# A decoder layer on one core: a simulated timeline for the scheduler's plan, a diagonal in a staging ring, shifted tiles, and a norm issued later

## The chip, the core and the metric

The kernel runs on one core of a Trainium2 chip. The metric is the device time of one execution in microseconds, as the median of repeated runs. A core has five engines that take their instructions in order: TensorE (PE, matmuls; PEld is its weight load), VectorE (DVE), ScalarE (ACT), GpSimd (POOL) and SyncE (SP, which here only issues DMAs). ACT and POOL issue DMAs too. Engines wait for each other through semaphores.

## The reference

One layer of a hybrid decoder in float32, on 1024 tokens of width 1024: a SwiGLU half, a mixer of stick-breaking attention beside a Mamba-2 state-space part (SSD), cross attention on 256 memory tokens, and a second SwiGLU half, each inside a pair of RMS norms.

```python
f = swiglu(rmsnorm(h, ffn1_pre_g), ffn1_w_gu, ffn1_w_down)
h = h + 0.5 * rmsnorm(f, ffn1_post_g)
m = hybrid_mixer(rmsnorm(h, mix_pre_g), w_in, ...)   # attention | SSD, each with a norm, then w_out
h = h + rmsnorm(m, mix_post_g)
c = memory_cross_attention(rmsnorm(h, xa_pre_g), rmsnorm(mem, mem_g), xa_wq, xa_wkv, xa_wo)
h = h + rmsnorm(c, xa_post_g)
f = swiglu(rmsnorm(h, ffn2_pre_g), ffn2_w_gu, ffn2_w_down)
h = h + 0.5 * rmsnorm(f, ffn2_post_g)
```

## The kernel before

Activations lie with features on the 128 partitions and tokens along the free axis, in two halves of 512 tokens (hh = 0, 1) and eight tiles of 128 features (d = 0 to 7). Every float32 product is made of three matmuls of a shorter type: an operand x is split into a high part (a cast, on ACT: L263 in `split`, L270 with a gain in `scaled_split`) and a low part (the rest, on DVE: L265 or L272). So "xh" and "xl" are the two parts of an activation, "whi" and "wlo" those of a weight, "hl", "dx", "ol", "atl" and the like other low or split parts. L138 is every matmul, L141 every transpose on TensorE.

The stages follow each other: the up phase of ffn1, its down product (`down_first`), the SSD with the in-projection, attention, the mixer's out-projection, cross attention (`xattn`), the up phase of ffn2 and its down product. In both up phases the larger part of the tiles is made with a scheme of seven block products (`seven`) instead of eight. It needs sums and differences of blocks: of weights on POOL (L737, into tiles "wc", then split by L263 and L265 into "whi", "wlo" or "blk") and of activations on ACT and DVE (`scale` L666, `combine` L676 and L679, into "bh" and "bl" in ffn1 and "wc" in ffn2, then split into "S", "xh", "xl"). L789 to L818, L649, L650 and L841 take products out of their banks and form the gate "ft"; L646 stores it.

**Order.** TensorE's order is written out by hand: `_pe` (L100) chains each matmul to the one before, keeps a clock of its own (`self.clock`, in ns, some 216 for a matmul of 512 columns), and runs whatever stands in `self.later` when that clock passes its time. The order on ACT, DVE, POOL and SP is chosen by the scheduler of the tile framework from its plan of the program, except that what is issued out of `self.later` keeps its place relative to its like (`kp`, L117). A tile is taken from a pool by a tag with `bufs` slots; which slot a tile gets, and so whose last reader it waits for, is part of that plan too.

**Norms.** A norm has three steps: sums of squares on ACT and DVE (`sumsq`: L378 and L381, then L382, and L384 that adds the two halves), `rms_cols`, eight small matmuls with a square root and reciprocal (L332 to L339), and `rms_rows`, which brings the factors to the partitions' layout: DVE splits them (L347, L348), writes two diagonals (L358; the first in "dg", the second in "low"), two matmuls with a matrix of ones sum them up, and ACT copies the result (L369, "rpre" or "rpost"). `post(0)` in `down_first` (L1114) does so for the first half of the tokens, by times given after the point where it is called: the columns at 12,000 ns, the rows at 15,500, and then a step every 4,700 from 17,500.

**The mixer row.** In attention's last pair of heads (p = 7), `inproj` has a ring "ev" of two slots in the pool sp. It holds keys taken out of a bank (L1719), differences of values that TensorE then transposes (L1726, the v tile), and eight raw tiles of the SSD's result that SP loads (L1790, from mix8 to mix15) and L270 and L272 split for the out-projection. `before(6)` makes the diagonals of the first mixer row (`mix_row(0)`, L1800), `before(8)` issues its product; a second row follows. Their second diagonal lies in the tile rpre0 or rpre1, which later takes the row itself.

Of the kernel before, what the change touches and what calls it, by code (L numbers as in the profile page):

```python
# [11 lines left out]
F32R = mybir.dt.float32r  # L12
# [6 lines left out]
P = 128  # L19
# [27 lines left out]
class Kern:  # L47
# [290 lines left out]
        if r2 is not None:  # L338
            self.kp(nc.vector.tensor_tensor(out=c, in0=c, in1=r2, op=ALU.mult))  # L339

    def rms_rows(self, c, home, behind=False):

        nc = self.nc
        nb = c.shape[1]
        cs = self.t(self.tp, [P, 16], F32R, "cs", bufs=1)
        ch, cl = cs[:, 0:nb], cs[:, 4 : 4 + nb]
        self.kp(nc.vector.tensor_copy(ch, c))  # L347
        self.kp(nc.vector.tensor_tensor(out=cl, in0=c, in1=ch.bitcast(F32), op=ALU.subtract))  # L348
        dg = self.t(self.tp, [P, 4, P], F32R, "dg", bufs=1)
        if isinstance(home, tuple):  # L350
            pool, tag = home
            low = self.t(pool, [P, 4, P], F32R, tag, bufs=1)[:, 0:nb, :]
        else:
            low = dg[:, nb : 2 * nb, :]
        parts = dg[:, 0:nb, :], low
        for o, x in zip(parts, (ch, cl)):
            self.kp(
                nc.vector.tensor_tensor(  # L358
                    out=o, in0=self.ident[:, :].unsqueeze(1).to_broadcast([P, nb, P]),
                    in1=x.bitcast(F32).unsqueeze(2).to_broadcast([P, nb, P]), op=ALU.mult,  # L360
                )
            )

        def product():
            ps = self.norm_bank()
            for i, x in enumerate(parts):
                self.mm(ps[:, 0 : nb * P], self.onesr, x.rearrange("p a b -> p (a b)"), i == 0, i == 1)
            r = self.t(pool, [P, H], F32, tag, bufs=1) if isinstance(home, tuple) else home
            self.kp(nc.scalar.copy(r, ps[:, 0 : nb * P]))  # L369
            return r  # L370

        return product if behind else product()
# [634 lines left out]
    def down_first(self, sp, rw, wdn, act_d, gpost, gnext):  # L1007


        nc = self.nc  # L1010
# [71 lines left out]
        accs = [self.new_accs(), None]  # L1082
# [28 lines left out]
        squares(0, 1, 4)  # L1111
        self.norm_pool = self.dnp, 4
        self.XH = [[self.t(self.xp, [P, H], F32R, f"xh{hh}{d}") for d in range(KT)] for hh in range(2)]
        self.post(0, gpost, self.C[0], gnext, step=4700, accs=accs[0], times=(12000, 15500, 17500), tail=(5500, 9000))  # L1114
        ps = banks(0)
        product(ps)
        self.norm_pool = self.msp, 1
# [534 lines left out]
    def attention(self):  # L1652
        nc, ap = self.nc, self.ap
        with self.pools("at", ["o", "a"], []) as (op, sp, pp):
# [130 lines left out]
            def before(n):  # L1785

                if n < 8:
                    k = n
                    raw = self.t(sp, [P, H], F32, "ev", bufs=2)
                    nc.sync.dma_start(out=raw, in_=self.mix_d[8 + k][:, 0:H])  # L1790
                    self.scaled_split(self.XH[0][k], self.XL[0][k], raw, self.par("ssd_norm_g", k))
                if n == 2:
                    ready.append(next(self.Wo))
                if n == 6:
                    late.append(mix_row(0))
                if n == 8:
                    late.pop()()

            def mix_row(i):
                product = self.rms_rows(self.norm_c[i][:, 0:4], (self.rp, f"rpre{i}"), True)  # L1800
                return lambda: self.mix_r.append(product())

            def scores(p, a, c):
# [138 lines left out]
            def beside():  # L1942
                late.append(mix_row(1))
                self.first = self.mix_first(ready.pop())
                for n in range(4 * MIXED):
                    if n == 2:
                        late.pop()()
                    if n == 4 * MIXED - 4:
                        ready.append(next(Wm))
                    next(self.first)  # L1950
                    yield
                yield from memory_values(*mem_prep())
# [128 lines left out]
    def xattn(self):  # L2081


        nc = self.nc
        with self.pools("xf", ["a", "b"], []) as (sp, sp2, pp):
# [23 lines left out]
            def scores(s):  # L2109

                KH, KL = K[s]
                p[s] = []
                if s % 4 == 0:
                    sc = self.t(self.rp, [P, 2, 4], F32, "sc")
                    scale[:] = sc[:, 0, :], sc[:, 1, :]
                    for x, f in zip(scale, (0.0625, -0.0625)):
                        nc.vector.tensor_scalar(out=x, in0=self.C[s // 4], scalar1=f, scalar2=None, op0=ALU.mult)
                for tb in range(4):
                    ts_ = slice(tb * P, (tb + 1) * P)
                    ps = self.t(pp, [P, 512], F32, "dn", bufs=3)[:, 0:MEM]  # L2120
                    self.mm3(ps, [(q[s][i][0][:, ts_], q[s][i][1][:, ts_], KH[:, i, :], KL[:, i, :]) for i in range(2)])
                    st = self.t(sp, [P, 2], F32, "st", bufs=4)
                    mx, sm = st[:, 0:1], st[:, 1:2]
                    e = self.t(sp, [P, MEM], F32, "p", bufs=4)
                    with self.urgent():
                        nc.vector.reduce_max(out=mx, in_=ps, axis=AX.X)
                        nc.vector.tensor_tensor(out=mx, in0=mx, in1=scale[1][:, tb : tb + 1], op=ALU.mult)
                        nc.scalar.activation(e, ps, AF.Exp, bias=mx, scale=scale[0][:, tb : tb + 1], accum_out=sm)
                        nc.vector.reciprocal(sm, sm)
                        nc.vector.tensor_scalar(out=e, in0=e, scalar1=sm, scalar2=None, op0=ALU.mult)  # L2130
                    p[s].append(e)
                    yield

            def values(s):
                VH, VL = V[s]
                if s == 0:
                    self.place(sp, 128)
                pT = [[self.t(sp, [P, H], F32R, f"pt{n}{m}", bufs=1) for m in range(2)] for n in range(2)]
                for tp in range(2):
                    tr = self.t(pp, [P, 2, 256], F32, "tr", bufs=1) if tp == 1 else self.t(self.msp, [P, 2, 256], F32, "ms", bufs=1)  # L2140
                    for m in range(2):
                        for tt in range(2):
                            self.tr(tr[:, m, tt * P : (tt + 1) * P], p[s][2 * tp + tt][:, m * P : (m + 1) * P])
                    c = slice(tp * 256, tp * 256 + 256)
                    with self.urgent():
                        for m in range(2):
                            self.split(pT[0][m][:, c], pT[1][m][:, c], tr[:, m, :])
                    yield
                for i in range(2):
                    ps = self.t(pp, [P, H], F32, "dn", bufs=3)  # L2150
                    c = slice(i * P, (i + 1) * P)
                    self.mm3(ps, [(VH[:, m, c], VL[:, m, c], pT[0][m], pT[1][m]) for m in range(2)])
                    hi = self.t(sp if s % 4 < 2 else sp2, [P, H], F32R, "oh", bufs=4)
                    lo = self.t(sp if s % 4 < 2 else sp2, [P, H], F32R, "ol", bufs=4)
                    with self.urgent():
                        self.split(hi, lo, ps)
                    o[s // 4].append((hi, lo))
                    yield

            def zip_(*gens):  # L2160
                gens = list(gens)
                while gens:
                    for x in list(gens):
                        try:
                            next(x)
                            yield
                        except StopIteration:
                            gens.remove(x)
# [24 lines left out]
            for s in range(8):  # L2193
# [19 lines left out]
                if s < 7:  # L2213
                    step = zip_(values(s), scores(s + 1))
# [5 lines left out]
                    else:  # L2220
# [3 lines left out]
                        self.merge(step, 6100, out_parts(0, 4), 5200)  # L2224
                    load(V, s + 1, "v", 1, 1)
            v = values(7)
            self.run_all(out_part(ps[0], ws[0], 1, 4, 6))
            next(v)
# [174 lines left out]
def build(arrays):  # L2403
    nc = bacc.Bacc("TRN2", target_bir_lowering=False, num_devices=1)
    ap = {
        n: nc.dram_tensor(f"in_{n}", v.shape, mybir.dt.from_np(v.dtype), kind="ExternalInput").ap()
        for n, v in arrays.items()
    }
    ap["out"] = [
        nc.dram_tensor(n, v, F32, kind="ExternalOutput").ap() for n, v in (("out_a", (H, D_MODEL)), ("out_b", (H, D_MODEL)))  # L2410
    ]
    with tile.TileContext(nc) as tc:
        Kern(nc, tc, ap).run()
    return nc

# [7 lines left out]
```

## Time and profile before

| | us |
|---|---|
| runs | 2644.43, 2643.67, 2641.38 (median 2643.67) |
| the profiled execution | 2645.18 |
| its span | 2643.4 |
| TensorE busy / idle in the span | 2576.9 / 66.5 |
| mean granted TensorE clock | 0.992 |
| POOL busy | 530.8 |

The span is what the trace covers; 1.8 us of the profiled execution lie around it. A row of the timeline gives start, duration, engine, line, operation, output and inputs, and in brackets the idle time of the engine before it with what ended it. Where matmuls overlap in the pipeline, the start to start distance counts (0.227 us for 128x512 at full clock), not the duration.

### The profile page before, as it was taken

To read this page: it belongs to the slowest core of one execution; us is meant where nothing else is said; L and a number is where in the kernel's file an instruction comes from. 1 tells how busy PE (TensorE), PEld (TensorE's weight loads), DVE (VectorE), ACT (ScalarE), POOL (GpSimd) and SP (SyncE) were. 2 spreads that over 40 slices of the span, in tenths; PEclk is the share of its full clock that TensorE was granted. 3 is DMA by queue.
4 is the path that set the end of the run, shared out by engine and by line. 5 is a ranking of instruction groups with operands and counts; after the bars stand their busy time and mean duration, and the time that the engine had idled before them with its cause. 6 is when DMAs were issued, how large, how long until landed. Compare 5 with 4: busy or idle time off the path is not lost.

```text
span 2643.4 us, 36454 instructions
## 1 busy us (share of the span) xinstructions
PE 2576.9 (97%) x12598; PEld 2135.0 (81%) x12598; DVE 1983.2 (75%) x3085; ACT 1262.9 (48%) x2276; POOL 530.8 (20%) x660
## 2 busy tenths in 40 slices
PE   8999999999999999999999998999999999999998
PEld 6788888887777778888888787887878788888887
DVE  7888787888678774777777777775448989895675
ACT  7544443545367783445554445254445433333432
POOL 1555552001100000000000001122012555542000
PEclk9999999999999999999999999999999999999999
DMA  5688887754721226433434458777667455555976
GB/s 209 238 308 302 304 282 252 255 193 158 259 79 45 71 70 196 115 99 108 109 108 115 146 178 323 252 274 252 218 230 272 167 187 203 195 180 210 347 276 218
DMA packets 225241, 528.87 MB, mean 200 GB/s; under 512 B 28064, under 2 KB 35104, under 8 KB 225056
## 3 DMA queue, kind: packets, MB, share of 16 engines
q1 hardware_dynamic: 190432, 419.56, 48.2%
q0 software_dynamic: 27424, 93.87, 9.8%
q10 hardware_dynamic: 7200, 13.11, 1.3%
q8 instruction: 99, 1.62, 0.3%
q14 instruction: 86, 0.70, 0.1%
HBM read 353.41 MB, written 152.04 MB: 191 GB/s over the span
## 4 chain that ended last, share of the span: by engine, by line
PE 79%; DVE 9%; DMA 6%; ACT 3%; issue 2%; POOL 1%; SPq 0%; DVEq 0%; ACTq 0%; POOLq 0%
PE mm L138 45%; PE dn L138 24%; PE z L138 2%; PE ms L138 2%; PE tr L141 2%; PE y L138 1%; PE ms L141 1%; DMA wraw<-act 1%; DMA raw<-act 1%; DVE hl L265 1%; DVE wlo L265 1%; PE seg L138 1%; DMA blk<-h 1%; DVE whi L265 0%; DMA oraw<-mix 0%
## 5 line engine op out<-in xcount | busy, mean ns | idle before, releaser
L138 PE MATMUL mm<-xh,whi 128*128 128x512 f32 x1288 | 511.5, 406 | 11.1 <-ACT xh L270 7.0
L138 PE MATMUL mm<-xh,wlo 128*128 128x512 f32 x1240 | 478.5, 393 | 3.2 <-DVE wlo L265 2.9
L138 PE MATMUL mm<-xl,whi 128*128 128x512 f32 x1188 | 467.8, 394 | 1.0 <-DVE xl L265 0.7
L138 PEld LDWEIGHTS mm<-xh,whi 128*128 128x128 f32 x1288 | 244.1, 189 | 53.6 <-ACT xh L270 6.9
L138 PEld LDWEIGHTS mm<-xh,wlo 128*128 128x128 f32 x1240 | 234.3, 189 | 55.3 <-DVE wlo L265 3.4
L138 PEld LDWEIGHTS mm<-xl,whi 128*128 128x128 f32 x1188 | 225.6, 190 | 34.1 <-DVE xl L265 1.8
L1823 DVE TENSOR_TENSOR_SCAN nb<-nb,begin 128x128 f32<-128x128 f32 (+7 forms) x128 | 171.7, 1352 | 55.0 <-ACT nb L1819 54.4
L1819 ACT ACTIVATE nb<-z,scale 128x128 f32<-128x128 f32 (+2 forms) x192 | 107.8, 580 | 88.8 <-PE z L138 87.7
L263 ACT CAST whi<-wraw 128x1024 fp32r<-128x1024 f32 (+1 forms) x89 | 81.2, 914 | 69.1 <-PE mm L138 39.1
L1856 POOL MEMSET ath<- 128x128 f32 x64 | 13.1, 205 | 499.0 <-PE mm L138 499.0
L265 DVE TENSOR_TENSOR wlo<-wraw,whi 128x1024 fp32r<-128x1024 f32 x61 | 74.4, 1220 | 38.3 <-ACT whi L263 38.0
L138 PE MATMUL dn<-xh,wlo 128*128 128x512 f32 x296 | 101.0, 389 | 0.0
L737 POOL TENSOR_TENSOR wc<-wraw,raw 128x512 f32<-128x512 f32 x57 | 87.5, 1535 | 66.6 <-DVE whi L265 30.7
L737 POOL TENSOR_TENSOR wc<-raw,wraw 128x512 f32<-128x512 f32 x55 | 85.5, 1555 | 66.5 <-DVE wlo L265 31.4
L819 POOL TENSOR_TENSOR ft<-ft,e 128x512 f32<-128x512 f32 x38 | 62.4, 1642 | 144.2 <-DVE e L818 85.7
L650 ACT ACTIVATE ft<-ft 128x512 f32<-128x512 f32 x88 | 55.4, 631 | 75.0 <-DVE ft L649 70.3
L263 ACT CAST ath<-tr 128x512 fp32r<-128x512 f32 (+1 forms) x107 | 58.2, 545 | 67.5 <-PE tr L141 66.1
L138 PE MATMUL dn<-xh,blk 128*128 128x512 f32 x280 | 90.2, 389 | 0.0
L265 DVE TENSOR_TENSOR atl<-tr,ath 128x512 fp32r<-128x512 f32 (+1 forms) x107 | 67.0, 629 | 29.2 <-ACT ath L263 28.9
L138 PE MATMUL dn<-xh,whi 128*128 128x512 f32 x256 | 88.0, 389 | 0.0
L138 PE MATMUL mm<-ath,v 128*128 128x256 f32 x320 | 86.2, 291 | 0.6 <-DVE sq L1838 0.6
L382 DVE TENSOR_TENSOR acc<-acc,sq 128x512 f32<-128x512 f32 x78 | 52.3, 684 | 42.5 <-ACT sq L381 42.2
(586 smaller groups left out, 6667.9 us busy)
## 6 DMA issues: line engine op xcount, KB each, us to landing
whi<-dwhi SPq DMA_DIRECT2D x57, 512.0 KB, 3.4
wlo<-dwlo SPq DMA_DIRECT2D x57, 512.0 KB, 4.2
wraw<-act SPq DMA_DIRECT2D x102, 256.0 KB, 4.4
raw<-act SPq DMA_DIRECT2D x96, 256.0 KB, 4.3
wraw<-in_w_gu SPq DMA_DIRECT2D x44, 512.0 KB, 4.4
raw<-in_w_gu SPq DMA_DIRECT2D x38, 512.0 KB, 4.8
khi<-whi POOLq DMA_DIRECT2D x30, 512.0 KB, 4.6
klo<-wlo POOLq DMA_DIRECT2D x30, 512.0 KB, 6.7
```

Source lines behind the costliest of these rows:

```text
L138: self._pe(self.nc.tensor.matmul(out, lhsT, rhs, start=start, stop=stop, skip_group_check=self.more), cost)
L141: self._pe(self.nc.tensor.transpose(out, src, self.ident if ident is None else ident), 109.0)
L263: self.kp(self.nc.scalar.copy(hi, src))
L265: (eng or self.nc.vector).tensor_tensor(out=lo, in0=src, in1=hi.bitcast(F32), op=ALU.subtract)
L382: self.kp(nc.vector.tensor_tensor(out=accs[i % 2], in0=accs[i % 2], in1=sq, op=ALU.add))
L650: nc.scalar.activation(t, t, AF.Silu)
L737: nc.gpsimd.tensor_tensor(out=t, in0=a, in1=b, op=op)
L819: nc.gpsimd.tensor_tensor(out=t1, in0=t1, in1=e, op=ALU.mult)
L1819: nc.scalar.activation(nb[:, s0:s1], z[:, 0:n], AF.Sigmoid, scale=sc[:, i : i + 1])
L1823: nc.vector.tensor_tensor_scan(out=nb[:, 0:Wd][:, ::-1], data0=nb[:, 0:Wd][:, ::-1], data1=begin[:, S - Wd : S][:, ::-1], initial=0.0, op0 ...
L1856: nc.gpsimd.memset(x[:, 0, :].bitcast(F32), 0.0)
```

## The change

Four things are changed. The tile framework's context is opened with a flag by which its scheduler makes its plan with a simulated timeline. `rms_rows` can take its second diagonal from a given pool's "ev" ring of two slots, and `mix_row` asks for that with attention's pool. `post(0)` in `down_first` issues its columns 4,500 ns later, its rows 3,000 later, starts its steps 3,000 later and makes them 400 shorter. `values` in cross attention sets aside 384 bytes a partition instead of 128, which moves the tiles allocated behind.

```diff
-    def rms_rows(self, c, home, behind=False):
+    def rms_rows(self, c, home, behind=False, at=None):
...
-            low = self.t(pool, [P, 4, P], F32R, tag, bufs=1)[:, 0:nb, :]
+            low = self.t(at or pool, [P, 4, P], F32R, "ev" if at else tag, bufs=2 if at else 1)[:, 0:nb, :]
...
-        self.post(0, gpost, self.C[0], gnext, step=4700, accs=accs[0], times=(12000, 15500, 17500), tail=(5500, 9000))
+        self.post(0, gpost, self.C[0], gnext, step=4300, accs=accs[0], times=(16500, 18500, 20500), tail=(5500, 9000))
...
-                product = self.rms_rows(self.norm_c[i][:, 0:4], (self.rp, f"rpre{i}"), True)
+                product = self.rms_rows(self.norm_c[i][:, 0:4], (self.rp, f"rpre{i}"), True, sp)
...
                 if s == 0:
-                    self.place(sp, 128)
+                    self.place(sp, 384)
...
-    with tile.TileContext(nc) as tc:
+    with tile.TileContext(nc, schedule_with_timeline_sim=True) as tc:
```

The flag changes the order on all engines but TensorE nearly everywhere: of some 3,060 rows on DVE 2,467 lines differ, on ACT 1,384 of some 2,180, on SP 978 of some 1,420, on POOL 231 of 649. TensorE keeps its sequence but for the norm that is issued later. Three places follow.

First, the mixer row (about 1470 us in the profile). The loads on SP of the raw tiles mix11 to mix14, with the semaphores that each waits for, before; "DVE" is the last reader of a slot by L272, "PE" TensorE's transposes of the v tile:

```order
L1790 DMA ev_3051_14472<-mix11_141 128x512 [waits DMAHW7_49,DMAHW1_49,DVE_49]
L1790 DMA ev_3055_14492<-mix12_142 128x512 [waits DMASW1_49,DMAHW4_49,DVE_49,PE_49]
L1790 DMA ev_3059_14509<-mix13_143 128x512 [waits DMAHW1_49,DVE_49]
L1790 DMA ev_3063_14538<-mix14_144 128x512 [waits DMAHW4_49,DVE_49,Activation_49]
L1790 DMA ev_3068_14557<-mix15_145 128x512 [waits DMAHW5_49,DMAHW3_49,DVE_49]
```

And with the change:

```order
L1790 DMA ev_3051_14472<-mix11_141 128x512 [waits DMAHW1_49,DMASW1_49,PE_49]
L1790 DMA ev_3055_14492<-mix12_142 128x512 [waits DMAHW1_49,DVE_49]
L1790 DMA ev_3059_14509<-mix13_143 128x512 [waits DMAHW4_49,DMAHW3_49,DVE_49]
L1790 DMA ev_3063_14538<-mix14_144 128x512 [waits DMAHW4_49,DVE_49]
L1790 DMA ev_3068_14557<-mix15_145 128x512 [waits DMAHW5_49,DMAHW6_49,PE_49,Activation_49]
```

The tile numbers are the same in both. Before, mix12's load waits for TensorE's transposes of the v tile, in the other slot than mix11; now it waits for DVE's read of mix11, in the same slot, and so on to mix14. On DVE, in the change, the rows from the scan (L1823) to the second split after the diagonals:

```order
L1823 SCALAR_TENSOR_TENSOR nb_3061_14530<-nb_3061_14530,begin_2088_9767 128x896
L272 SCALAR_TENSOR_TENSOR xl0_1335_6161<-ev_3051_14472,params_3_78,xh03_1248_5794 128x512
L272 SCALAR_TENSOR_TENSOR xl0_1343_6206<-ev_3055_14492,params_3_78,xh04_1249_5795 128x512
L272 SCALAR_TENSOR_TENSOR xl0_1353_6255<-ev_3059_14509,params_3_78,xh05_1250_5796 128x512
L272 SCALAR_TENSOR_TENSOR xl0_1356_6286<-ev_3063_14538,params_3_78,xh06_1251_5797 128x512
L358 TENSOR_TENSOR ev_3066_14546<-ident_36_112,cs_3064_14542 128x512
L347 CAST cs_3089_14658<-cy1_2082_9742 128x4
L348 TENSOR_TENSOR cs_3089_14658<-cy1_2082_9742,cs_3089_14658 128x4
L358 TENSOR_TENSOR dg_3090_14661<-ident_36_112,cs_3089_14658 128x512
L1823 SCALAR_TENSOR_TENSOR nb_3069_14561<-nb_3069_14561,begin_2088_9767 128x1024
L265 TENSOR_TENSOR atl_3076_14581<-tr_3074_14579,ath_3075_14580 128x512
```

The second diagonal of the first row (ev_3066) follows the L272 of mix14 (ev_3063), into the slot which that frees; before, it lay in rpre0, and none of these four L272 stood between the scan and the diagonal of the second row (dg_3090).

Second, ffn1's up phase (about 92 to 104 us). ACT's rows before; bh_295 is the last sum of activations for the product that runs, wc_309 to wc_320 are sums of weights from POOL for the next ones:

```order
L666 ACTIVATE blk_289_945<-blk_289_945,params_3_78 128x512
L263 CAST blk_301_1010<-wc_300_1008 128x512
L263 CAST xh12_14_90<-bl_290_952 128x512
L263 CAST blk_304_1029<-wc_303_1027 128x512
L263 CAST xh13_15_91<-bh_295_982 128x512
L263 CAST blk_307_1049<-wraw_278_875 128x512
L263 CAST whi_310_1070<-wc_309_1068 128x512
L263 CAST whi_317_1113<-raw2_277_873 128x512
L263 CAST wlo_313_1091<-wc_312_1089 128x512
L263 CAST wlo_321_1134<-wc_320_1132 128x512
```

And with the change:

```order
L263 CAST blk_301_1010<-wc_300_1008 128x512
L263 CAST xh12_14_90<-bl_290_952 128x512
L263 CAST blk_304_1029<-wc_303_1027 128x512
L263 CAST whi_310_1070<-wc_309_1068 128x512
L263 CAST whi_317_1113<-raw2_277_873 128x512
L263 CAST wlo_313_1091<-wc_312_1089 128x512
L666 ACTIVATE blk_289_945<-blk_289_945,params_3_78 128x512
L263 CAST wlo_321_1134<-wc_320_1132 128x512
L263 CAST xh13_15_91<-bh_295_982 128x512
L263 CAST blk_307_1049<-wraw_278_875 128x512
```

The scaling for the last sum (L666) went behind three weight casts, and its cast (xh13) behind four; on DVE its sum (L679 bh_295) stands behind the same three and its low part (xl1_31) behind the fourth.

Third, ffn2's up phase (about 2041 to 2053 us), DVE's rows with the change; ft_4351 is a gate whose second factor comes from bank mm_4361, wc_4346 and wc_4356 are sums of activations of which the next matmuls need xl0_4069 and xl0_4083:

```order
L841 TENSOR_TENSOR ft_4351_19897<-ft_4351_19897,mm_4361_19951 128x512
L265 TENSOR_TENSOR whi_4374_20026<-wraw_4332_19794,whi_4374_20026 128x512
L265 TENSOR_TENSOR S12_4276_19469<-wc_4340_19828,S12_4276_19469 128x512
L679 SCALAR_TENSOR_TENSOR wc_4341_19840<-blk_4324_19747,params_3_78,blk_4323_19744 128x512
L679 SCALAR_TENSOR_TENSOR wc_4345_19858<-blk_4324_19747,params_3_78,blk_4323_19744 128x512
L265 TENSOR_TENSOR S42_4280_19473<-wc_4341_19840,S42_4280_19473 128x512
L265 TENSOR_TENSOR S52_4284_19477<-wc_4345_19858,S52_4284_19477 128x512
L679 SCALAR_TENSOR_TENSOR wc_4346_19869<-blk_4324_19747,params_3_78,blk_4323_19744 128x512
L265 TENSOR_TENSOR xl0_4069_18937<-wc_4346_19869,xh06_1251_5797 128x512
```

Before, L841 of ft_4351 stood ten rows behind xl0_4069, between S53 (the sum after) and wc_4356; it is now ahead of S12.

## The prediction

> **What bounds it now.** I read the page first: who is busy, and of whom the chain that ended last is made.
>
> ```profile
> PE 2576.9 (97%) x12598; PEld 2135.0 (81%) x12598; DVE 1983.2 (75%) x3085; ACT 1262.9 (48%) x2276; POOL 530.8 (20%) x660
> PE 79%; DVE 9%; DMA 6%; ACT 3%; issue 2%; POOL 1%; SPq 0%; DVEq 0%; ACTq 0%; POOLq 0%
> ```
>
> TensorE is idle for 2643.4 − 2576.9 = 66.5 us, and its matmuls are not touched by the change. So the change is worth the waits that it takes from TensorE or adds to it, and what each does to the clock. The table of stretches shows the clock.
>
> ```profile
> core 0: us, PE busy (x) PEld busy (x) DVE busy (x) ACT busy (x) POOL busy (x), PEclk, DMA share, GB/s
> 84.00:97.00 13.00, 11.47 (x48) 8.10 (x46) 12.73 (x18) 7.94 (x14) 6.27 (x7) 1.00 0.78 271
> 612.00:624.00 12.00, 8.92 (x28) 6.94 (x29) 11.50 (x25) 7.83 (x15) 0.00 (x0) 0.72 0.36 111
> 1484.00:1490.00 6.00, 2.19 (x5) 1.39 (x6) 4.64 (x8) 2.65 (x4) 0.00 (x0) 0.50 0.35 97
> 1490.00:1500.00 10.00, 10.00 (x49) 8.59 (x48) 4.47 (x8) 3.62 (x8) 0.67 (x4) 0.80 0.59 190
> 1788.00:1800.00 12.00, 9.36 (x37) 7.68 (x38) 5.71 (x14) 2.49 (x6) 1.07 (x2) 0.86 0.61 208
> ```
>
> PEclk below 1 is time at half speed: a stretch of 12 us at 0.72 lost 12 × 0.28 = 3.4 us, 12 us at 0.86 lost 1.7, and after 1484 some 10 us ran at half (6 × 0.50 + 10 × 0.20 = 5.0 lost). These are the places of longer waits. In 84 to 97, DVE is busy 12.73 of 13 us: there VectorE, and not TensorE, sets the pace. ACT and DVE take their rows in order, so a row that is moved ahead and must wait holds up all rows behind it; the order of the two programs shows where that happens.
>
> **The mixer row's second diagonal (about 1470 to 1490).** Rows of the timeline and of the load's line:
>
> ```profile
> 1471.80 2.00 DVE L1823 TENSOR_TENSOR_SCAN nb<-nb,begin 128x896 f32<-128x896 f32 x1
> 1472.10 0.39 PE L138 MATMUL ms<-rpre,onesr 128*128 128x512 f32 x1
> 1473.16 0.42 PEld L141 LDWEIGHTS ms<-ident,ev 128*128 128x128 f32 x4
> 1473.74 0.65 DVE L358 TENSOR_TENSOR dg<-ident,cs 128x512 fp32r<-128x512 f32 x1
> 1483.84 0.80 PE L138 MATMUL ms<-dg,onesr 128*128 128x512 f32 x1 [1.90 <-DVE atl L265]
> 1488.45 0.79 PE L138 MATMUL ms<-rpre,onesr 128*128 128x512 f32 x1 [3.81 <-DVE rpre L358]
> 1489.04 0.63 PE L138 MATMUL mm<-xh,whi 128*128 128x512 f32 x1
> DMA to landing us min/median/max: 2.6/3.0/4.3
> L270 ACT ACTIVATE xh<-ev,params x8: 712/722/727, 1458.0 to 1486.3; 128x512 fp32r<-128x512 f32 x8
> L272 DVE SCALAR_TENSOR_TENSOR xl<-ev,params,xh x8: 724/750/752, 1459.0 to 1487.0; 128x512 fp32r<-128x512 f32 x8
> ```
>
> Before, the first row's second matmul (1472.10) waits for nothing. After, its operand is a tile of the "ev" ring, and the ring has two slots. One is held by the v tile that TensorE transposes at 1473.16, behind this matmul in its order. So the raw tiles of mix11 to mix14 and then the diagonal go through the other slot one by one: each load waits until L272 has read the tile before. The first L272 can start when the scan ends (1471.80 + 2.00) and ends at 1474.55. Then three times a landing of 3.0 us, L270's 0.72 and L272's 0.75: 3 × 4.47 = 13.4, to 1487.95; the diagonal (L358, 0.65) makes it 1488.6. TensorE is ready at 1472.10: **a wait of 16.5 us** (15.3 with landings of 2.6, 20.4 with 4.3).
>
> From 1472.10 TensorE then has 9.84 us of work up to the second row's first matmul (1483.84 less its wait of 1.90), 0.46 for that row, and about 4.5 us are lost at half clock (5.0 were lost behind the 1484 wait, which was shorter): 1488.6 + 14.8 = 1503.4 for what stood at 1489.04, +14.4. The old waits of 1.90 and 3.81 are in that difference. What half clock cost behind 1489.04 before (0.5 + 2.0) does not come again. **+12**, bounds +9.5 and +16.
>
> The Trainium skill's page "DMA: Bandwidth & Descriptors", section "Anatomy of one DMA — SWDGE (gpsimd) path", gives a fixed 2.0 us plus bytes over 436 GB/s, which for these 256 KB is an estimate of 2.6 us. The trace agrees for the quickest landing only; by the page this part would be 1.2 us cheaper, by the median row it is as above, and the row decides.
>
> **ffn1's operand sums (92 to 104).**
>
> ```profile
> 92.65 0.72 ACT L666 ACTIVATE blk<-blk,params 128x512 f32<-128x512 f32 x1 [1.99 <-DMA blk<-in_xT]
> 93.41 0.75 DVE L679 SCALAR_TENSOR_TENSOR bh<-blk,params 128x512 f32<-128x512 f32 x1
> 95.64 0.68 DVE L265 TENSOR_TENSOR xl<-bh,xh 128x512 fp32r<-128x512 f32 x1
> 96.38 0.51 PE L138 MATMUL mm<-xl,whi 128*128 128x512 f32 x1 [0.24 <-DVE xl L265]
> 98.16 1.61 POOL L737 TENSOR_TENSOR wc<-wraw,raw 128x512 f32<-128x512 f32 x1 [0.70 <-ACT whi L263]
> 98.54 1.77 DVE L265 TENSOR_TENSOR whi<-wc,whi 128x512 fp32r<-128x512 f32 x1
> 100.40 1.29 POOL L737 TENSOR_TENSOR wc<-raw,wraw 128x512 f32<-128x512 f32 x1 [0.63 <-DVE whi L265]
> 101.72 0.62 ACT L263 CAST wlo<-wc 128x512 fp32r<-128x512 f32 x1 [1.30 <-POOL wc L737]
> ```
>
> Before, the last operand sum of the product (92.65, 93.41) goes ahead of four weight casts; after, it stands behind them on both engines. The last cast needs POOL's third sum (100.40 to 101.69). It can be earlier by the two DVE rows taken out ahead of it (0.75 + 0.68 = 1.4): it ends at 100.3, the cast at 100.9, then xh (0.62) and xl behind a wlo row (0.68 to 1.77, then 0.68) end at 102.3 to 103.4. TensorE took it at 96.38: **+6.4** at a start near 102.8 (bounds +5 and +8.5, the latter with no earlier POOL). Half clock behind such a wait costs at least 1.7, as at 1788: together **+8**, bounds +5 and +11. At the start of the program squares and sums now stand among the first splits: up to 5 DVE rows of 0.6 = 3 us. DVE sets the pace until 97, so most of it is lost in the wait just priced: **+1** (0 to +4).
>
> **ffn2's operand sums (2042 to 2063)**, the same pattern with another blocker:
>
> ```profile
> 2041.43 0.74 DVE L679 SCALAR_TENSOR_TENSOR wc<-blk,params,blk 128x512 f32<-128x512 f32 x1
> 2046.10 0.39 PE L138 MATMUL mm<-xh,wlo 128*128 128x512 f32 x1
> 2049.42 0.68 DVE L841 TENSOR_TENSOR ft<-ft,mm 128x512 f32<-128x512 f32 x1
> 2051.95 1.28 DVE L265 TENSOR_TENSOR xl<-wc,xh 128x512 fp32r<-128x512 f32 x2
> 2052.69 0.50 PE L138 MATMUL mm<-xl,wlo 128*128 128x512 f32 x1 [0.71 <-DVE xl L265]
> 2055.33 0.72 ACT L666 ACTIVATE blk<-blk,params 128x512 f32<-128x512 f32 x1 [2.29 <-DMA blk<-h]
> 2086.33 2.07 PE L138 MATMUL mm<-S,whi 128*128 128x512 f32 x4 [3.83 <-DVE e L798]
> ```
>
> L841 reads a bank whose last matmul ends at 2046.49. Before, it is taken at 2049.42, behind the sum of 2041.43; after, that sum is the eighth row from L841 on: 2046.5 + 8 × 0.62 = 2051.5, about 0.8 later where ACT's casts between them wait in turn, so 2052.3 for what ended at 2042.17. From there to the end of the next operand (the first of the two xl rows, 2052.63) it took 10.46 us. Six rows of 0.6 that stood between are now ahead of it, which leaves at least 6.9, and 8.3 with the alternation of ACT and DVE: 2060.6, **+8**, bounds +6.5 and +10. The load that ACT waits for at 2055.33 is issued when this sum's tile is read, so it shifts along. The half clock behind this wait is charged nothing: the wait of 3.83 at 2086 hides it, and 3.4 is due without it.
>
> **The first norm of down_first (612 to 624) and the moved cast in xattn.**
>
> ```profile
> L138 PE MATMUL dn<-dg,onesr 128*128 128x512 f32 x1 | 0.5, 502 | 0.9 <-DVE dg L358 0.9
> L138 PE MATMUL dn<-small,acc 128*128 128x1 f32 x8 | 1.9, 355 | 4.7 <-DVE acc L384 4.7
> 613.34 0.68 DVE L384 TENSOR_TENSOR acc<-acc,acc 128x512 f32<-128x512 f32 x1
> 613.94 0.68 DVE L265 TENSOR_TENSOR whi<-xl,whi 128x512 fp32r<-128x512 f32 x1
> 1789.37 1.22 DVE L265 TENSOR_TENSOR wlo<-wraw,whi 128x1024 fp32r<-128x1024 f32 x1
> 1790.64 0.50 PE L138 MATMUL mm<-xh,wlo 128*128 128x512 f32 x1 [2.95 <-DVE wlo L265]
> L336 ACT ACT_TABLE_LOAD x10 | 12.8, 1283 | 0.9 <-PE ms L138 0.7
> ```
>
> The column sums move back by 4.5 us of the plan's clock, 21 matmuls or some 4.7 us: alone this would take 4.7 + 0.9 and the 3.4 of half clock, −9. But DVE's L384 (613.34) moves behind seven more rows of 0.60 (613.34 to 613.94), 4.2 us, and the matmuls between columns and rows go from 16 to 9, so the second wait grows by about 1. **0**, bounds −9 and +3. In xattn the wlo cast of 1789.37 is 42 rows earlier: −2.95 and −1.7 of clock; against it, that cast (1.22) and rows of 0.68 now stand ahead of the split of pt that TensorE takes at once, about +2. **−2.7**, bounds −4.7 and +2; the 384 bytes only shift tiles. ACT gets three more table loads of 1.28 us, which its idle half of the span covers (3.8 at most where it doesn't). In all other places rows move by a few ranks; I put them at 0, with −6 and +10.
>
> On the clock, the Trainium skill's "TensorE: Matmul & The Clock Gate", Part 1, lets the clock halve after an idle window of about 3.4 us. The wait of 2.95 us here is shorter and still lost 1.7: the trace disagrees, and the row decides; by the page the cast would be worth 2.95 and the sum 1.7 higher.
>
> **The sum.** 12 + 8 + 1 + 8 + 0 − 2.7 + 0 = +26.3. It is made against the profiled run, 2645.18, 1.5 above the median shown: 2671.5 there, 2670 beside the median.
>
> **Rivals.**
> - *The engines run ahead.* If ACT and DVE reached the rows moved ahead 7 to 16 us sooner than in before, the three long waits vanish, and the first norm (−9), the old waits of the mixer row (−5.7 and −5 of clock) and the cast (−4.7) are won: 2643.7 − 24 = 2619. It decides at the point where a load of mix12 is issued without waiting for the tile before it. For it: DVE is idle a quarter of the span. Against it: the slot is held until 1473.16, and ACT idles at 92.65 and 2055.33 for transfers, so the casts wait for their inputs. 5%.
> - *The gains cover it.* The first norm comes off whole and ffn2's sums are hidden: 12 + 8 + 1 − 9 − 4.7 = +7, and with the mixer row and ffn1 at their lower bounds +1: 2645. For it speaks that the 21 matmuls are certain; against it, that L384 moves too. 8%.
> - *More places bind.* The same in-order wait stands in other stages, by ten places of 1 to 2 us: 2685. For it: 66.5 us of idle time lie in many short waits, at whose places DVE is already last. Against it: at many of them the rows keep their order. 20%.
> - That the plan does not change is excluded by the order: 2467 lines of difference on DVE.
>
> **How the numbers follow.** The forecast of 2670 has 67%. The range takes the sum of the likelier halves of the bounds, about −22 and +21: 2648 to 2691. A measurement of this kernel tells 0.2% (5.3 us) from no change. Faster 0.06 (the first rival and a little of the second), same 0.06, slower 0.88.
>
> **What would show it.** A PE row "ms<-ev" near 1472 with a wait of 15 us or more whose releaser is DVE L358, and L1790 loads 4 to 5 us apart: if that wait is under 5, the largest term is wrong. An mm<-xl wait of 5 us or more near 97 to 104 and another near 2053 to 2062, if not, those terms go. At 612 a wait for L384 of 3 to 5 us: if it is gone, −9. No wait for wlo near 1790. A PE idle sum near 66.5 + 25 with more half clock would confirm the sum.

## The result: 2.7% slower, lost in many short waits

The changed kernel takes 2714.97 us (median of 4 runs, 2711.44 to 2718.25); before, beside it, takes 2644.05 (4 runs, 2641.38 to 2646.38). The ratio is 1.0268, with a 95% interval from 1.0251 to 1.0286. The profiled execution took 2713.81 us, its span is 2712.0, the mean granted clock 0.981. The page of the changed kernel has these lines for the two of before:

```profile
PE 2596.7 (96%) x12598; PEld 2146.4 (79%) x12598; DVE 1973.3 (73%) x3085; ACT 1268.9 (47%) x2279; POOL 535.3 (20%) x660
PE 76%; DVE 8%; DMA 5%; issue 4%; ACT 4%; POOL 1%; SPq 0%; DVEq 0%; ACTq 0%; POOLq 0%
```

They give the two halves of the loss. TensorE is idle for 2712.0 − 2596.7 = 115.3 us, 48.8 more than before. It does the same 12,598 matmuls, yet is busy for 19.8 us more: more of them ran at half clock. 48.8 + 19.8 = 68.6, the difference of the spans. DVE and ACT are as busy as before, so no engine got more work. The table of stretches shows where the clock went:

```profile
core 0: us, PE busy (x) PEld busy (x) DVE busy (x) ACT busy (x) POOL busy (x), PEclk, DMA share, GB/s
28.00:40.00 12.00, 8.22 (x22) 5.77 (x21) 8.08 (x15) 7.99 (x13) 0.00 (x0) 0.72 0.07 24
94.00:101.00 7.00, 5.47 (x13) 4.32 (x14) 5.74 (x7) 3.49 (x6) 4.15 (x5) 0.52 0.84 258
111.00:118.00 7.00, 5.31 (x12) 3.87 (x13) 5.91 (x7) 2.81 (x5) 3.94 (x3) 0.51 0.48 135
780.00:801.00 21.00, 16.13 (x71) 12.65 (x71) 11.12 (x23) 16.44 (x36) 0.00 (x0) 0.84 0.07 26
1002.00:1030.00 28.00, 22.08 (x126) 17.66 (x126) 17.18 (x38) 17.95 (x33) 0.00 (x0) 0.82 0.23 79
1524.00:1532.00 8.00, 5.33 (x23) 4.78 (x24) 5.30 (x8) 3.93 (x7) 0.00 (x0) 0.56 0.31 98
2109.00:2125.00 16.00, 7.41 (x19) 4.78 (x18) 12.11 (x18) 8.52 (x14) 5.51 (x9) 0.68 0.51 170
```

In the SSD no engine is full (780 to 801, 1002 to 1030: DVE and ACT are busy for 53 to 78% of the time), and still 3.4 and 5.0 us are lost to the clock (21 × 0.16 and 28 × 0.18). Rows of the timeline at the waits:

```profile
30.20 0.47 PE L138 MATMUL ms<-dg,onesr 128*128 128x512 f32 x1 [1.74 <-DVE dg L358]
111.86 0.80 PE L138 MATMUL mm<-xh,whi 128*128 128x512 f32 x1 [5.12 <-ACT xh L263]
780.09 2.15 ACT L1409 ACTIVATE rb<-csr,params 128x128 fp32r<-128x128 f32 x7 [5.60 <-DVE csr L1385]
782.15 0.24 ACT L1401 COPY Bl<-seg 128x128 f32<-128x128 f32 x1
782.45 0.49 PE L138 MATMUL seg<-Ct,Bt 128*128 128x128 f32 x2 [2.43 <-ACT Bl L1401]
1005.84 1.22 PE L138 MATMUL st<-xdec,Bl 128*128 128x256 f32 x2 [2.02 <-DVE xdec L1444]
1024.35 0.63 PE L138 MATMUL ms<-dg,onesr 128*128 128x256 f32 x2 [3.16 <-DVE dg L358]
1044.51 2.87 DVE L1523 TENSOR_TENSOR yacc<-yacc,sq 128x512 f32<-128x512 f32 x4
1047.30 0.42 DVE L1560 TENSOR_TENSOR sq<-mm,Ct 128x256 f32<-128x256 f32 x1
1047.86 0.36 PE L138 MATMUL mm<-xs,whi 128*128 128x256 f32 x1 [3.33 <-DVE sq L1560]
1516.72 0.75 DVE L272 SCALAR_TENSOR_TENSOR xl<-ev,params,xh 128x512 fp32r<-128x512 f32 x1 [3.28 <-ACT xh L270]
1520.99 0.75 DVE L272 SCALAR_TENSOR_TENSOR xl<-ev,params,xh 128x512 fp32r<-128x512 f32 x1 [3.52 <-ACT xh L270]
1525.14 0.75 DVE L272 SCALAR_TENSOR_TENSOR xl<-ev,params,xh 128x512 fp32r<-128x512 f32 x1 [3.40 <-ACT xh L270]
1525.92 0.69 DVE L358 TENSOR_TENSOR ev<-ident,cs 128x512 fp32r<-128x512 f32 x1
1526.67 0.80 PE L138 MATMUL ms<-ev,onesr 128*128 128x512 f32 x1 [14.86 <-DVE ev L358]
1668.68 0.77 PE L138 MATMUL ms<-dg,onesr 128*128 128x512 f32 x1 [7.19 <-DVE dg L358]
2119.41 0.79 PE L138 MATMUL mm<-xh,wlo 128*128 128x512 f32 x1 [5.89 <-ACT xh L263]
```

Two of them show the pattern, a row that TensorE waits for behind rows that it does not wait for. At 780, ACT has waited for csr and takes seven copies (L1409, "rb") ahead of the copy Bl (L1401), for which TensorE has stood still since 782.45 − 2.43 = 780.02. At 1044, DVE adds four squares of the SSD's gate (L1523), whose sum TensorE reads only at 1053.7, ahead of L1560, the row that frees TensorE's bank.

To see where the 68.6 us arise, take the start of each matmul in a run less the start of the same matmul in before. How much this shift grows in each stretch of before's time, in us (stretches that an edit does not touch still differ by up to some 2.6, as 1510 to 1640 does in e7; 130 to 600 and 690 to 750 add nothing in any of them):

| before's time | changed | e1: flag alone | e2: edits, no flag | e9: flag, old order on ACT, DVE | e12: and on TensorE |
|---|---|---|---|---|---|
| 0 to 50, start | +5.9 | +5.1 | −0.1 | +5.7 | −0.6 |
| 50 to 130, ffn1 | +11.7 | +7.5 | +0.5 | +0.5 | −0.3 |
| 600 to 690, first norms | −2.0 | −1.9 | +2.8 | +0.7 | −2.7 |
| 750 to 1075, SSD | +19.9 | +22.2 | +0.7 | +2.2 | +1.9 |
| 1075 to 1465, attention | +4.3 | +3.0 | −0.2 | −0.1 | 0.0 |
| 1465 to 1510, mixer row | +9.5 | −1.4 | +9.1 | −0.4 | −0.1 |
| 1510 to 1640, mixer's product | +2.7 | +3.6 | −2.5 | −1.6 | −0.1 |
| 1640 to 1800 | +1.8 | +2.4 | −1.5 | +1.1 | 0.0 |
| 1800 to 2000, cross attention | +4.1 | +3.6 | 0.0 | −0.2 | +0.1 |
| 2000 to 2070, ffn2's start | +11.1 | +9.0 | +1.4 | +8.5 | −1.3 |
| 2070 to 2120 | −3.8 | −1.5 | −2.8 | −2.2 | −1.4 |
| 2120 to the end | +3.6 | +4.1 | −0.4 | +4.6 | +4.4 |
| sum | +68.6 | +55.7 | +7.0 | +18.8 | −0.2 |

Matmuls are matched by the program's names. The expectation of e12 below has +7.0 and +7.2 for e9's start and ffn2's; matched so they are +5.7 and +8.5.

### The profile page after: what moved, and what is told of

The parts are those of the page before. It is cut to its first block, busy times and chain, and to the rows that moved or that the text cites. A ratio compares the mean times of both kernels' runs of the same rounds, so it can differ in the third digit from the quotient of the medians.

```text
span 2712.0 us, 36454 instructions
## 1 busy us (share of the span) xinstructions
PE 2596.7 (96%) x12598; PEld 2146.4 (79%) x12598; DVE 1973.3 (73%) x3085; ACT 1268.9 (47%) x2279; POOL 535.3 (20%) x660
## 4 chain that ended last, share of the span: by engine, by line
PE 76%; DVE 8%; DMA 5%; issue 4%; ACT 4%; POOL 1%; SPq 0%; DVEq 0%; ACTq 0%; POOLq 0%
PE mm L138 41%; PE dn L138 26%; PE z L138 2%; PE ms L138 2%; PE tr L141 2%; PE ms L141 1%; PE y L138 1%; DMA wraw<-act 1%; DMA raw<-in_w_dn 1%; DVE wlo L265 1%; DMA raw<-act 1%; DMA xl<-h 1%; PE seg L138 1%; DVE hl L265 0%; DVE whi L265 0%
## 5 line engine op out<-in xcount | busy, mean ns | idle before, releaser
L1823 DVE TENSOR_TENSOR_SCAN nb<-nb,begin 128x128 f32<-128x128 f32 (+7 forms) x128 | 171.9, 1353 | 58.1 <-ACT nb L1819 57.4
L138 PE MATMUL mm<-atl,v 128*128 128x256 f32 x320 | 83.1, 281 | 1.1 <-DVE atl L265 1.1
```

Of the source, the lines that this page charges most:

```text
L138: self._pe(self.nc.tensor.matmul(out, lhsT, rhs, start=start, stop=stop, skip_group_check=self.more), cost)
L1823: nc.vector.tensor_tensor_scan(out=nb[:, 0:Wd][:, ::-1], data0=nb[:, 0:Wd][:, ::-1], data1=begin[:, S - Wd : S][:, ::-1], initial=0.0, op0 ...
```

## The experiments

**The flag alone, and the edits without it (e1, e2).**

```diff
# e1: before, with
+    with tile.TileContext(nc, schedule_with_timeline_sim=True) as tc:
# e2: the changed kernel, with
+    with tile.TileContext(nc) as tc:
```

> The kernel before with the flag alone. Theory P (plan): the order that the simulated timeline gives costs the time by itself, in many places; then 2690 to 2720, with the waits near 111 us, in the SSD between 1003 and 1050 us and in ffn2 as in the changed kernel, and without the wait of 14.9 us at the mixer row. Rival E (edits): the three edits cost it and the flag alone is near neutral; then 2640 to 2665. Rival J (joint): the flag costs half and the ring tile under the flag the rest; then 2665 to 2690.

> The changed kernel with the flag taken out, so the three edits alone. Theory P: within 10 us of before, 2634 to 2654; the later norm takes up to 9 us, the ring tile gives up to 8 back. Rival E: 2690 or more, with a wait over 10 us at the mixer row. Rival J: 2644 to 2660.

e1 took 2701.98 us, ratio 1.0234 [1.0209, 1.0259]; e2 2652.84, ratio 1.0044 [1.0027, 1.0062]. So the flag is by far the larger part, and nearly every stretch of the table has its shift from it. One has not: the mixer row. The timeline of e2:

```profile
1490.94 0.80 PE L138 MATMUL ms<-ev,onesr 128*128 128x512 f32 x1 [15.05 <-DVE ev L358]
```

The wait is there without the flag, and absent with the flag alone (−1.4). It belongs to the edit, not to the plan.

**One edit taken back, under the flag (e3, e4).**

```diff
# e3: the changed kernel, with the second diagonal in its old tile
+                product = self.rms_rows(self.norm_c[i][:, 0:4], (self.rp, f"rpre{i}"), True)
# e4: the changed kernel, with the first norm's old times
+        self.post(0, gpost, self.C[0], gnext, step=4700, accs=accs[0], times=(12000, 15500, 17500), tail=(5500, 9000))
```

> The changed kernel with the second diagonal back in its own tile; the flag, the norm's times and the 384 bytes stay. By the trace of the changed kernel the mixer row cost 8.7 us against before (shift 40.5 to 49.2 between 1462 and 1504 us of before). Theory P: the wait of 14.9 us for L358 goes, the rest stays: 2715 - 9 = 2706, not below 2698. Rivals E and J: 2690 or less.

> The changed kernel with the norm's old times (columns at 12000, rows at 15500, steps of 4700 from 17500). By the trace the region of the first norm (593 to 636 us of before) gained 3.1 us net under the flag, 6.6 at the columns less 3.5 at the rows. Theory P: 2715 + 3 = 2718, range 2712 to 2724, a wait of 4 us or more for L384 back near 630. If the later norm is what costs (rival E): below 2706.

e3: 2699.75, ratio 1.0215 [1.0189, 1.0241]; e4: 2716.19, ratio 1.0282 [1.0264, 1.0301]. The ring costs 2714.97 − 2699.75 = 15 us (12 by the profiles, 68.6 − 56.6); the norm's times change the whole by no more than the runs scatter.

**The mixer row: later use of the ring tile; and the norm's times, alone (e6, e7, e8).** e6 has the ring and the 384 bytes but not the flag, and TensorE takes the first row's product behind the transposes of the second v tile, which free the other slot. e7 and e8 are before with other times in `post(0)`.

```diff
# e6: before with the ring edit and 384 bytes, and in the loop over n
+                    if p == 7 and n < 5:
...
+                        if p == 7 and n == 5:
+                            late.pop()()
-                if n == 8:
-                    late.pop()()
# e7
+        self.post(0, gpost, self.C[0], gnext, step=4300, accs=accs[0], times=(16500, 18500, 20500), tail=(5500, 9000))
# e8
+        self.post(0, gpost, self.C[0], gnext, step=3700, accs=accs[0], times=(16500, 24500, 26500), tail=(5500, 9000))
```

> The kernel before with the ring tile (and the 384 bytes), no flag, old times, and the first mixer row's product issued behind the transposes of the v tile instead of ahead of them. Slot theory (the ring's other slot is held by the v tile until TensorE transposes it, so all loads and the diagonal queue through one): with the transposes first, both slots turn; the wait of 15 us falls under 4, the old waits of 1.9 and 3.8 mostly go, 2633 to 2644. Rival (the loads themselves are too slow for the place, or the ring is one tile too small whatever the order): still a wait of 10 us or more, 2650 or more.

> The kernel before with the norm's new times alone, no flag. In the run of the three edits without the flag the columns waited for nothing and the rows 6.8 us, the next norm 5.9 us (2.5 before). If this is the edit's own doing: the same two waits, 2642 + 3 = 2645, range 2641 to 2650. If it came of the ring or the bytes: the waits of before, or a gain of up to 9: 2633 to 2641.

> The kernel before with the columns at 16500, the rows at 24500 and steps of 3700 from 26500, no flag: rows 37 matmuls behind the columns instead of 9. If the rows' wait of 6.8 us is DVE's order between columns and rows (some 15 rows of 0.6 us ahead of the norm's), the 8.4 us hide it: waits under 1 us at both, 2642 - 8 = 2634, range 2630 to 2640; the next norm may take 2 to 5 of it back by the denser steps. If DVE is simply behind by then, the wait moves to the steps or the next norm: 2640 to 2650.

e6: 2644.77, ratio 1.0015 [1.0006, 1.0025]. The wait falls from 15.05 to 8.76 us, not below 4, and the stretch from +9.1 to +3.8: holding the slot explains about half of it. Of the rest, 2.8 us pass until DVE's scan (L1823) ends at 1473.2, and three rows of L272 still stand between it and the diagonal, of which the last waits 2.27 us for its high part on ACT. e7: 2642.86, ratio 1.0005 [0.9995, 1.0016]: at the first norm TensorE waits 5.84 us for dg (L358), where it waited 4.70 for acc (L384) and 0.91 for dg, and at the second 5.01 for acc, where it waited 2.54. Issuing the norm later moved the wait from the columns to the rows. e8: 2637.65, ratio 0.9985 [0.9975, 0.9995], the first version faster than before, by 0.15%. Its waits, in the timeline:

```profile
626.50 0.80 PE L138 MATMUL dn<-dg,onesr 128*128 128x512 f32 x1 [2.77 <-DVE dg L358]
669.65 1.65 PE L138 MATMUL ms<-small,acc 128*128 128x1 f32 x7 [6.38 <-DVE acc L384]
1787.12 0.79 PE L138 MATMUL mm<-xh,wlo 128*128 128x512 f32 x1 [2.93 <-DVE wlo L265]
```

With the rows 9 us later too, the first norm gains 4.8 us by 645; at the second one, 669, most comes back (+4.3), since its sum hangs on rows that now come later.

**ffn1's order of sums, under the flag (e5).** The splits of the second weight tile keep their place behind the operand sums, as in before.

```diff
# e5: before with the flag, and in the seven block products
+                was, self.inlater = self.inlater, self.inlater or (f == PLAIN + 1 and begin is not None)
...
+                self.inlater = was
```

> The kernel with the flag alone, with the splits of the second weight tile of ffn1's block products kept behind the activations' operand sums that were issued before them (their order on ACT and DVE is taken from the program). Theory P, first step (rows moved ahead of an operand sum hold it up): the wait for xh and xl near 95 to 113 goes, and of the 7.6 us that the flag alone cost between 80 and 130 us at least 5 go; 2702 - 6 = 2696, the region at +3 or less. Rival L (the loads land later under the flag, whatever the order on ACT and DVE): the region stays at +6 or more, as a wait at the same sums.

2697.51, ratio 1.021 [1.0193, 1.0226]. The order did turn round, and the shift in 50 to 130 stayed: +6.8 where at most +3 was expected (e1: +7.5). In e1 TensorE waits here for 1.28, 1.36 and 5.12 us; in e5 the 5.12 is 2.41, and the 1.28 has become 2.60:

```profile
94.27 0.50 PE L138 MATMUL mm<-xl,wlo 128*128 128x512 f32 x1 [2.60 <-DVE xl L265]
106.86 0.80 PE L138 MATMUL mm<-xh,whi 128*128 128x512 f32 x1 [2.41 <-ACT xh L263]
96.20 1.10 POOL L663 DMA_DIRECT2D blk<-in_xT  x2 [0.85 <-DVE bl L679]
104.28 0.72 ACT L666 ACTIVATE blk<-blk,params 128x512 f32<-128x512 f32 x1 [1.94 <-DMA blk<-in_xT]
```

The chain is late before that place: POOL issues the load of the last tile when DVE has read the tile before it, and both of its users come after. Taking one inversion away lets the next one bind. By its number the run fits the rival in the expectation, loads that land later whatever the order on ACT and DVE; e9 below speaks against that, since there the loads keep the flag's order on SP and POOL, and this stretch has +0.5.

**The old order of rows, imposed under the flag (e9, e10, e11).** If the plan's order is the cause, the flag with before's order must be as fast as before. A list of before's rows, by name, is chained: a row may not be issued ahead of its predecessor in the list.

```diff
# e9: before with the flag; the list holds all rows of ACT and DVE
# e10: only the SSD's, 358 of ACT and 407 of DVE.   e11: all of DVE's
+        at = {i.name: i for i in nc.cur_bb.bb.instructions}
...
+            if prev is not None:
+                tc.add_manual_dep(at[name], prev, NOSYNC, reason="order of another plan")
+            prev = name
```

> Theory O: the flag costs through the order in which the plan puts ACT's and DVE's rows, since both take them in order. With the flag on, but all rows of ACT and DVE chained in the order of before, nearly all of the +57 us of the flag alone must go: 2640 to 2655. Theory T: it costs through what the plan decides besides, that is the slots of tiles, the order of loads on SP and POOL (774 and 169 lines of difference) and the places of the norms' small matmuls on TensorE (165 lines), which all stay as with the flag: then half or more of the +57 stays, 2675 or above.

> The same chain for the SSD alone: 358 rows of ACT and 407 of DVE, from the first convolution row to the end of the last chunk; the rest of the program has the order of the flag. Theory O: the shift gained between 750 and 1075 us of the time before, +22 with the flag alone, falls to +5 or less, and the time to 2680 to 2688 (2702 less 17 or so). Theory T: the shift there stays at +15 or more and the time at 2695 or above.

> DVE's rows alone in the order of before, ACT's as the flag puts them. If DVE's order is what costs, the time is near that of both engines in the old order, 2660 or less; if ACT's is, near the flag alone, 2690 or more. I expect both to matter, since the waits of the flag alone name DVE (xl, dg, v) about as often as ACT (xh, Bl): 2665 to 2690.

e9: 2660.82, ratio 1.0065 [1.0048, 1.0082]. e10: 2686.84, ratio 1.0167 [1.0151, 1.0183]. e11: 2701.61, ratio 1.0223 [1.0206, 1.024]. In e10 the SSD's shift falls from +22.2 to +1.8: the SSD's loss is the order of ACT's and DVE's rows there. In e9 all but 18.8 of the profile's +55.7 are gone: less is left than theory T says, more than theory O (2640 to 2655). e11 was expected between 2665 and 2690 and gives nothing at all: DVE in the old order with ACT in the new one keeps +19.9 in the SSD. ACT makes the high part or the copy and DVE the rest, in turns, which would explain that one order alone is worth nothing. But ACT's order alone was not tried, so it is open whether both are needed or ACT's would do.

**What stayed in e9 (e12).** It stayed in two places, the start and ffn2's start, where ACT and DVE have the old order. The timeline at the start, of before:

```profile
22.62 0.95 PE L138 MATMUL ms<-small,acc 128*128 128x1 f32 x8
25.24 0.18 DVE L337 RECIPROCAL cpre<-cpre 128x4 f32<-128x4 f32 x1 [1.77 <-ACT cpre L336]
```

and of e9:

```profile
26.68 0.95 PE L138 MATMUL ms<-small,acc 128*128 128x1 f32 x8
29.30 0.18 DVE L337 RECIPROCAL cpre<-cpre 128x4 f32<-128x4 f32 x1 [5.92 <-ACT cpre L336]
31.67 0.77 PE L138 MATMUL ms<-dg,onesr 128*128 128x512 f32 x1 [3.70 <-DVE dg L358]
```

The eight small matmuls of the norm (`rms_cols`; four in the program, each two records in the trace) are four microseconds later on TensorE, so the factors are, so the diagonal is, and TensorE waits for it. These matmuls are not in the hand-written chain: the plan places them. Under the flag alone 35 matmuls of the program stand elsewhere on TensorE: 20 of these, 13 products of a norm's rows with the matrix of ones, which are not in the chain either, and 2 others. For example, before and then (+) with the flag:

```order
 L138 MATMUL mm_418<-xh_6_82,whi_281 128x512
-L138 MATMUL ms_260<-small_114,acc_87_236 128x1 x4
 L138 MATMUL mm_418<-xl_22_98,whi_281 128x512
...
 L138 MATMUL mm_418<-xh_10_86,whi_281 128x512
+L138 MATMUL ms_260<-small_114,acc_87_236 128x1 x4
 L138 MATMUL mm_418<-xl_26_102,whi_281 128x512
```

At ffn2 the same: TensorE takes the small matmuls of the norm of cross attention at 1980.81 in before and 1993.35 in e9, POOL then issues the last stores of h and the loads of what was stored. Before, and then e9:

```profile
2003.49 1.14 POOL L437 DMA_DIRECT2D h<-F  x2 [2.12 <-DVE F L432]
2013.30 3.18 POOL L663 DMA_DIRECT2D blk<-h  x6 [7.55 <-DMA h<-F]
```

```profile
2017.58 1.14 POOL L437 DMA_DIRECT2D h<-F  x2 [2.14 <-DVE F L432]
2025.46 3.18 POOL L663 DMA_DIRECT2D blk<-h  x6 [4.65 <-DMA h<-F]
2067.09 0.79 PE L138 MATMUL mm<-xh,wlo 128*128 128x512 f32 x1 [4.84 <-ACT xh L263]
```

TensorE itself is about 8 us later there, the stores and loads 12 to 14, and the difference is the wait of 4.84. e12 chains TensorE's rows too (the same diff, the list with PE).

> As the run with ACT's and DVE's rows in the old order, and now TensorE's rows too; what is left of the flag is the order on SP and POOL (781 and 177 lines) and the slots. Theory F: the +16 us that stayed there are the norms' small matmuls, which are not chained on TensorE and which the flag's plan puts 10 to 40 rows later (at the start the norm's factors came 4 us later, in cross attention the stores of h and all loads behind them 14 us later). Then the shift before 50 us (+7.0) and between 2000 and 2070 us (+7.2) is gone and the time is 2642 to 2650. Theory T: it is the order of loads on SP and POOL and the slots; both shifts stay and the time is 2656 or above.

2646.17, ratio 1.0027 [1.0015, 1.0039], in the range of theory F: both shifts are gone (−0.6 and −1.3). In ratios, the flag's 2.34% falls to 0.65% with ACT's and DVE's order and to 0.27% with TensorE's. The last 0.27% are left to slots and to the order on SP and POOL; the +4.4 behind 2120, which every run with the flag has (3.4 to 4.6), may be part of it. In e12's trace most of it lies at 2430 to 2439, in short waits of TensorE (0.2 to 0.6 us each) for halves of weights that ACT and DVE split, and ACT waits there for the loads (raw and wraw). What makes them late was not sought.

**The cause used the other way (e13).** Without the flag: e8, and on DVE rows nobody waits for put behind rows that TensorE waits for.

```diff
# e13: e8, and
+        for first, then in MOVES:
+            for n in then:
+                tc.add_manual_dep(at[f"I-{n}"], f"I-{first}", NOSYNC, reason="rows moved behind on VectorE")
...
+MOVES = (
+    (17478, (17387, 17398, 17425, 17433)),   # wlo cast in cross attention; L272, L382 of the norm
+    (17434, (17580,)),                       # L384; a later split
+    (20204, (20304, 20321)),                 # L798 in ffn2; two splits
+)
```

> No flag and none of the other edits: the first norm's rows later (the run that was 0.15% faster than before), and rows that TensorE does not need at once moved behind rows that it waits for, on DVE: in cross attention four rows of the norm (L272, L382) behind the wlo cast of which TensorE waits 2.9 us at 1787, in ffn2 two splits (2.9 and 1.8 us long there) behind L798, for which it waits 3.8 us at 2082. If such waits end with the row that is last in DVE's order, both go, with their half clock: 1.7 to 2.9 and 1.7 + 3.8, so 2637.7 - 9 = 2629 (2625 to 2634). If what stands behind is as late, 2634 to 2642.

2631.36 (before, beside it, 2640.20), ratio 0.9966 [0.9953, 0.9978]: 0.34% faster than before, and in the range expected of "both go". But only one went, so the number fits in part by luck. TensorE waits no longer for wlo, and from 1745 to 1800 the shift is −4.8. In ffn2 the wait for L798 at 2082 is gone and another for the next L798 has come, seventeen us on:

```profile
2098.82 1.65 PE L138 MATMUL dn<-S,blk 128*128 128x512 f32 x3 [3.17 <-DVE e L798]
```

From 2000 to 2120 the shift is −1.7, where e8 had −0.8: the wait was passed on, not removed.

## Why the prediction was wrong in size

The direction was right, the size was not: +26 was forecast, +71 came.

- **The step that failed** is "In all other places rows move by a few ranks; I put them at 0, with −6 and +10." Those places gave +34.6: the SSD 19.9, attention 4.3, the mixer's product 2.7, cross attention 4.1, the end 3.6. e10 shows the SSD's to be the order of ACT's and DVE's rows, e9 nearly all the rest but the end (the wait of 7.19 at 1668 is gone there). Why the simulated timeline puts the rows so was not tried. A few ranks are enough: in the SSD one copy behind seven others is 2.4 us of wait and 1.7 lost to half clock behind it (783.4 to 786.8).
- **The rival "more places bind"** (2685, 20%) named this. Its ten places of 1 to 2 us were too few, and it charged no half clock: of the 68.6 us, 19.8 are clock.
- **A premise was wrong too**: "its matmuls are not touched by the change". Their work is not, their order is: the norms' matmuls are placed by the plan, so it is also wrong that under the flag TensorE keeps its sequence but for the first norm. By e9 and e12 this is the start (+5.9, forecast +1) and ffn2's start.
- **The mixer row** (+12, wait 16.5): +9.5, wait 14.86. Three rounds through one slot took 4.01, 4.27 and 4.15 us from one L272 to the next, where 4.47 was forecast: the loads (L1790, issued on SP) landed after 2.5 to 2.9 us, nearer to the quickest of before, 2.6, than to the 3.0 that the sum used. The mechanism was right, but the plan has no part in it: e2 has the wait without the flag.
- **ffn1's sums** (+8): +11.7. The wait of 5.12 stands where it was foreseen; a second one of 2.60 at 95, with its own 3.4 us lost to half clock, was not.
- **ffn2's sums** (+8): +11.1, and −3.8 behind 2070, where the half clock was indeed already due. The size was near by chance: I put it on DVE's order, and e9, which has the old order there, keeps 8.5 of it. Whether DVE's order alone would cost as much was not tried.
- **The first norm** (0): −2.0, close, but not in the way forecast, so this is luck. A wait for L384 of 3 to 5 us was to stay at the columns. It is gone, and the −9 did not come: TensorE waits 3.44 us for the rows' dg, where it waited 0.91, and at the second norm 4.56 for acc, where it waited 2.54. e7 shows the same move of the waits without the flag.
- **The cast in cross attention** (−2.7): the wait for wlo is gone, and TensorE gains 4.9 there, but just ahead of it, at 1825 and 1828, came two waits of 1.89 and 1.95 us for the split of pt, which with their half clock cost 6.1. Together +1.2: the +2 that was set against the gain was too small.

## What to carry to other kernels

Where a scheduler's plan changes as a whole, price the number of short waits it can make, not the few long ones that the order shows: count the places where an engine that takes rows in order has, ahead of a row that TensorE waits for, rows that nobody waits for. See which rows of the bounding engine are chained and which the plan may place; a norm's eight small matmuls, placed 4 us later, cost some 6 us at the start. To find out whether an order is the cause, impose the old order on one engine after the other, and on pairs: here DVE's order alone left the loss at 2.23% of 2.34%, ACT's and DVE's together at 0.65%.

## What the runs showed of the hardware

Waits of nearly the same length cost half clock in one place and none in another. The stretches of the table, of before, around waits of 1.70 us (776.40) and 1.64 us (839.51):

```profile
776.00:781.00 5.00, 4.60 (x18) 3.31 (x19) 2.93 (x9) 4.97 (x12) 0.00 (x0) 0.66 0.00 0
839.00:844.00 5.00, 4.49 (x30) 3.54 (x31) 5.00 (x13) 4.52 (x12) 0.00 (x0) 1.00 0.00 0
```

and of the changed kernel, around three waits of 1.97 us in attention (1207.68, 1330.71, 1393.01):

```profile
1207.00:1214.00 7.00, 6.32 (x40) 5.61 (x41) 5.31 (x12) 3.48 (x7) 0.00 (x0) 1.00 0.64 183
1330.00:1337.00 7.00, 6.29 (x40) 5.56 (x41) 5.30 (x11) 3.48 (x7) 0.00 (x0) 1.00 0.64 181
1393.00:1400.00 7.00, 6.99 (x36) 6.05 (x36) 4.72 (x9) 2.46 (x6) 0.00 (x0) 0.76 0.55 143
```

A clock of 0.66 over 5 us and of 0.76 over 7 are 3.4 us at half speed, 1.7 us lost. In these traces the half-speed stretches inside the span last 3.4 us or multiples of it (6.8, 10.2, 17.1). A wait of under 2 us can cost 1.7 us more, and its length alone doesn't tell whether it does. The Trainium skill's "TensorE: Matmul & The Clock Gate", Part 1, describes a free-running window of about 3.4 us over which activity is watched; the lengths, and that waits of one length differ, agree with it; where in such a window a wait lay, no run here shows. Its section "HAM oscillation — how this bites in real kernels" allows idle gaps up to about 3.4 us; here 1.70 us were too long.
